# A ConvGLU block on one Trainium2 core: seven column pairs by seven products, and operand halves formed by transfers

## The chip, the cores and the metric

The kernel runs on one core of a Trainium2 chip. Its engines are TensorE (PE, matmuls), VectorE (DVE), ScalarE (ACT), GpSimd (POOL) and SyncE (SP); each runs its own queue of instructions in order, and semaphores order them against each other. Matmul results land in PSUM, everything else in SBUF. Transfers (DMAs) are sent from a queue of SP, POOL or ACT and then run by themselves. The metric is the time of one execution on the device in microseconds (us).

## The reference, cut to what matters

One layer of an encoder block over 512 tokens of width 1024: a combined projection, two attention branches, a gated merge, and a convolutional GLU. The change concerns the last part alone:

```python
def conv_glu(x, w_up, conv_w, conv_b, w_down):        # x: 512 x 1024, normalized
    hid = x @ w_up                                    # 1024 -> 2 * 2816
    hid = causal_depthwise_conv(hid, width=3) + conv_b
    gate, up = hid[..., :2816], hid[..., 2816:]
    return (silu(gate) * up) @ w_down                 # 2816 -> 1024
...
x = x + conv_glu(rms_norm(x, norm2_g), w_ffn_up, ffn_conv_w, ffn_conv_b, w_ffn_down)
```

All of it is in float32, to float32 accuracy. TensorE reads a rounded format (fp32r), so the kernel splits each operand a into a high half hi = round(a) and a low half lo = a − hi, and forms each product as three: hi·hi, hi·lo and lo·hi.

## The kernel before

**Chunks.** The weights come as a list of chunks. `load(i)` sends the transfer of chunk i from SP into a buffer `raw` (two of them); `split_gen(i)` makes `whi` (by ACT's copy) and `wlo` (by DVE's subtraction) of it, sends the load of chunk i + 2 and then yields. `run_chunk` runs the body of one chunk on PE, and at each yield of the body takes one step of the next chunk's split. So PE works on chunk i while ACT and DVE split chunk i + 1 and the load of i + 2 is under way.

**Up projection.** There are 22 column pairs, up0 to up21: 128 gate columns and the 128 up columns that belong to them. An ordinary pair (`up_body`) has 48 matmuls of 128x512. A pair in `SEVEN` (`up_seven`) is computed by Strassen's scheme in Winograd's form: the 1024 x 256 weights and the tokens are cut in two each way, and seven products of blocks take the place of eight, with sums of blocks as operands: 84 matmuls of 128x256. The sums on the token side (`ts`, four tiles, `token_sums`) are made once from a transposed copy that went through DRAM (`htd`); their splits into halves are taken during two ordinary pairs. The sums on the weight side are made for each such pair by DVE: `block_sums` (tile `sx` and one in place in `raw`), and `split_seven` splits them into `wxh` and `wxl`. Partial products are added in `pc`, `hg` and `hu`. Before, `SEVEN` is (5, 8, 11, 14, 17).

**After each pair**, `up_fin` and `gate` apply the convolution (one ACT instruction and two on DVE for each half), silu on ACT into `cg`, and DVE's product into `ub`, which holds four of them.

**Operands of the down projection.** The down projection is computed by seven products as well. For this, each two column pairs 2i and 2i + 1 give an operand pair i (0 to 10): `ax` (the blocks that the first half needs) and `ay` (those of the second). `pair_sums(i)` makes them: four sums of blocks on DVE into `st` (one buffer) and `ub`, then halves: for each part of `ax` and `ay` a cast on ACT into the first half of the tile, and a subtraction on DVE (L909) into the second. The steps of operand pairs 0 to 8 are written right behind `up_fin`. Since SBUF is short, `ay` of pairs 0 to 6 is spilled to DRAM (`ayd`), by a DMA on POOL's queue, and fetched back by `fetch`, also on POOL's queue: five after up18, two inside the down projection.

**Down projection.** The first half, dn0, runs over 11 chunks dn0_0 to dn0_10 of 24 matmuls of 128x512, with `ax`; the second, dn1, over 11 chunks of 18 with `ay`. The weights' own sums are made in `split_down` (in `raw`, kept in t, "t2_..."), first the sums, then the first lo half, the second, and t. A load of dn0_n goes out when chunk n − 2 has let go of its buffer (dn0_2 has one of its own).

**What sets the order.** The code is written for a scheduler that orders each engine's instructions; `behind(a, others)` puts an order between two instructions without a wait, and `chain` does so along a list: in dn0 DVE's and ACT's split work runs along such chains (`late["halves"]`, `late["casts"]`), whose first links (at n = 1) stand behind the last product of up21 (`late["fin"]`) and its last tap. Tiles wait for the last use of the buffer that they take over.

Of the kernel before, what the change touches and what calls it, by code (L numbers as in the profile page):

```python
# [8 lines left out]
F32 = mybir.dt.float32  # L9
# [53 lines left out]
SEVEN = (5, 8, 11, 14, 17)  # L63
# [3 lines left out]
def block_kernel(ctx: ExitStack, tc: tile.TileContext, x, xt, params, g2, rbx, wts, wd0, wd1, out):  # L67
# [45 lines left out]
    def load(i, parts=1):  # L113
# [6 lines left out]
        if i >= FIRST_DN:  # L120
            n = i - FIRST_DN
            if n < NP:
                SP.dma_start(raw, wd0[n])
            else:
                late["load"] = (SP.dma_start(raw[:, 0:1024], wd1[n - NP]),)
            yield
            return

        cuts = [0, *parts, 8] if isinstance(parts, tuple) else [8 * j // parts for j in range(parts + 1)]
        for a, b in zip(cuts, cuts[1:]):  # L130
            sl = slice(256 * a, 256 * b)
            SP.dma_start(raw[:, sl], wts[i, :, sl])
            yield
# [39 lines left out]
    def block_sums(i):  # L173

        b = raws[i].rearrange("p (b c) -> p b c", c=512)
        sx = late["pool"].tile([P, 1536], F32, tag="sx", name=f"sx_{order[i]}")
        late["sx"] = sx
        s1, s2, s4 = (sx[:, 512 * j:512 * (j + 1)] for j in range(3))
        V.tensor_tensor(s1, b[:, 1], b[:, 3], op=ALU.add)
        yield  # L180
        V.tensor_tensor(s2, s1, b[:, 0], op=ALU.subtract)
        yield
        V.tensor_tensor(s4, b[:, 2], s2, op=ALU.subtract)
# [4 lines left out]
    def split_seven(i, raw, hi, lo):  # L188

        key = order[i]  # L190
# [3 lines left out]
        sx = late["sx"]  # L194
        for j, (h, l, src) in enumerate(((hi[:, 0:1024], lo[:, 0:1024], raw[:, 0:1024]),
                                         (wh[:, 0:1024], wl[:, 0:1024], sx[:, 0:1024]),
                                         (hi[:, 1024:2048], lo[:, 1024:2048], raw[:, 1024:2048]),
                                         (wh[:, 1024:1536], wl[:, 1024:1536], sx[:, 1024:1536]))):
            A.copy(h, src)
            V.tensor_tensor(l, src, h.bitcast(F32), op=ALU.subtract)  # L200
            if j < 3:
                yield
# [62 lines left out]
    ayd = dram.tile([7, P, 1536], F32, tag="ayd", name="ayd")  # L265

# [354 lines left out]

    def soft_b(h, t, ps):
# [247 lines left out]
    def pair_sums(i):  # L870
# [5 lines left out]
        if i < 8:  # L876
            ax = fp.tile([P, 2048], F32R, tag="ax", name=f"ax{i}", bufs=8)
            ay = fp.tile([P, 1536], F32R, tag="ay", name=f"ay{i}")
        elif i == 8:

            ax = fp.tile([P, 2048], F32R, tag="ts", name=f"ax{i}", bufs=4)
            ay = fp.tile([P, 1600], F32R, tag="wxh", name=f"ay{i}")[:, 0:1536]
            keep[0] = fp.tile([P, S], F32, tag="hg", name="t2_0")
# [367 lines left out]
```

## Time and profile before

| | |
|---|---|
| median of 3 runs | 726.2 us (725.96 to 726.39) |
| profiled execution | 726.66 us, its span 724.9 us |
| PE / DVE / ACT / POOL busy | 718.6 / 565.4 / 401.5 / 53.6 us |
| up projection, pairs 2 to 21 with the rest of 0 and 1 | 403.0 to 615.8 us |
| down projection, dn0 and dn1 | 615.8 to 675.6 and to 720.8 us |
| transferred | 100.91 MB, 139 GB/s on average |

How to read the rows: a group gives the line of the kernel, the engine, the operation, what it writes and reads with sizes, and how often (x), then busy us in all, mean ns of one, idle time of the engine just before, and what ended that idle time. A row of the chain of waits gives a start in us, a length, and the work. A row of the timeline gives start, length and the work, with idle time ahead of it in brackets; x2 stands for two instructions in one row. A row of transfers gives count, size and the median time from issue to landing. A row of windows gives the busy time of each engine in a stretch, with the granted clock of PE (1.00 is full speed), the busy share of the DMA engines, and GB/s.

### The profile page before, as it was taken

The page shows a single profiled execution, that of the slowest core. Times are in us where ns is not written, and L with a number is a line of the kernel's source. Part 1 is how long each engine was busy: PE and PEld are TensorE (multiplying, and loading weights), DVE is VectorE, ACT ScalarE, POOL GpSimd, SP SyncE. Part 2 cuts the span into 40 slices and gives each one's busy share as a digit, 9 for nine tenths or more (in the row PEclk, how much of TensorE's full clock was granted, in tenths as well). Part 3 has the DMA queues.
Part 4 walks back from the last instruction along what each step waited for, and adds up shares of the span by engine and source line. Part 5 has one row for each costly group of instructions (what it writes and reads, how often), then busy time and mean ns, then how long its engine had stood idle before and what let it go on. Part 6 is the DMA issues. An engine that isn't in the chain of part 4 may idle for free.

```text
span 724.9 us, 10589 instructions
## 1 busy us (share of the span) xinstructions
PE 718.6 (99%) x4019; PEld 627.5 (87%) x4019; DVE 565.4 (78%) x1030; ACT 401.5 (55%) x727; POOL 53.6 (7%) x95
## 2 busy tenths in 40 slices
PE   8999999999999999999999999999999999999997
PEld 8999998888988888888889889889898988888886
DVE  6678867775988888566275799998979985997686
ACT  6675656657767676442254556655545653543541
POOL 2701200000101011000012000000000100000000
PEclk9999999999999999999999999999999999999999
DMA  8632232211313111314536613544335553564563
GB/s 308 250 131 78 83 117 74 74 59 58 118 63 113 59 59 59 136 68 144 195 149 239 203 62 156 186 135 160 118 145 186 181 184 117 173 243 174 177 222 116
DMA packets 24786, 100.91 MB, mean 139 GB/s; under 512 B 2592, under 2 KB 7328, under 8 KB 17184
## 3 DMA queue, kind: packets, MB, share of 16 engines
q1 hardware_dynamic: 21792, 87.00, 33.8%
q0 software_dynamic: 2656, 13.11, 5.0%
q8 instruction: 31, 0.51, 0.3%
q14 instruction: 19, 0.16, 0.1%
q10 hardware_dynamic: 288, 0.14, 0.1%
HBM read 88.44 MB, written 11.80 MB: 138 GB/s over the span
## 4 chain that ended last, share of the span: by engine, by line
PE 98%; DMA 1%; SPq 0%; DVE 0%; ACT 0%; DVEq 0%; issue 0%
PE P L1087 14%; PE p L998 7%; PE pg L254 4%; PE pg L253 4%; PE pg L255 4%; PE pu L254 4%; PE pu L255 4%; PE pu L253 4%; PE qkB L255 2%; PE gB L255 2%; PE qkB L253 2%; PE gA L253 2%; PE gA L254 2%; PE gB L253 2%; PE gA L255 2%; PE qkB L254 2%
## 5 line engine op out<-in xcount | busy, mean ns | idle before, releaser
L253 PE MATMUL pg<-hth,whi_up 128*128 128x512 f32 (+1 forms) x152 | 55.7, 367 | 0.0
L255 PE MATMUL pg<-hth,wlo_up 128*128 128x512 f32 (+1 forms) x152 | 55.7, 366 | 0.0
L254 PE MATMUL pg<-htl,whi_up 128*128 128x512 f32 (+1 forms) x152 | 55.7, 366 | 0.0
L254 PE MATMUL pu<-htl,whi_up 128*128 128x512 f32 (+1 forms) x152 | 55.6, 366 | 0.0
L253 PE MATMUL pu<-hth,whi_up 128*128 128x512 f32 (+1 forms) x152 | 55.6, 366 | 0.0
L255 PE MATMUL pu<-hth,wlo_up 128*128 128x512 f32 (+1 forms) x152 | 55.6, 365 | 0.0
L1087 PE MATMUL P<-whi_dn,ax 128*128 128x512 f32 x176 | 54.4, 389 | 0.0
L149 ACT CAST whi_dn<-raw_dn 128x1024 fp32r<-128x1024 f32 x33 | 34.3, 1051 | 25.5 <-PE P L1087 15.2
L145 DVE TENSOR_TENSOR wlo_dn<-raw_dn,whi_dn 128x1024 fp32r<-128x1024 f32 x33 | 40.0, 1224 | 9.2 <-ACT whi_dn L149 9.1
L228 DVE TENSOR_TENSOR wlo_up<-raw_up,whi_up 128x1024 fp32r<-128x1024 f32 (+1 forms) x40 | 41.2, 1062 | 7.0 <-ACT whi_up L226 7.0
L226 ACT CAST whi_up<-raw_up 128x1024 fp32r<-128x1024 f32 (+1 forms) x40 | 34.5, 917 | 14.7 <-PE pu L254 7.9
L1087 PE MATMUL P<-whi_dn,ay 128*128 128x512 f32 x132 | 40.8, 389 | 0.0
L1087 PEld LDWEIGHTS P<-whi_dn,ax 128*128 128x128 f32 x176 | 33.0, 188 | 6.8
L1087 PE MATMUL P<-wlo_dn,ax 128*128 128x512 f32 x88 | 34.2, 389 | 0.0
L254 PEld LDWEIGHTS pu<-htl,whi_up 128*128 128x128 f32 x152 | 28.6, 188 | 4.7
L253 PEld LDWEIGHTS pu<-hth,whi_up 128*128 128x128 f32 x152 | 28.5, 188 | 4.7
L255 PEld LDWEIGHTS pg<-hth,wlo_up 128*128 128x128 f32 x152 | 28.6, 188 | 4.7
L255 PEld LDWEIGHTS pu<-hth,wlo_up 128*128 128x128 f32 x152 | 28.5, 188 | 4.6
L253 PEld LDWEIGHTS pg<-hth,whi_up 128*128 128x128 f32 x152 | 28.6, 188 | 4.6
L254 PEld LDWEIGHTS pg<-htl,whi_up 128*128 128x128 f32 x152 | 28.6, 188 | 4.5
L633 DVE TENSOR_TENSOR_SCAN aB<-aB,reset 128x127 f32<-128x127 f32 (+3 forms) x32 | 26.0, 817 | 6.7 <-ACT aB L628 6.7
L1087 PEld LDWEIGHTS P<-whi_dn,ay 128*128 128x128 f32 x132 | 24.8, 188 | 5.1
(303 smaller groups left out, 2240.3 us busy)
## 6 DMA issues: line engine op xcount, KB each, us to landing
raw_up<-in_wts SPq DMA_DIRECT2D x22, 1024.0 KB, 4.8
raw_dn<-in_wd SPq DMA_DIRECT2D x11, 1024.0 KB, 4.8
raw_dn<-in_wd SPq DMA_DIRECT2D x11, 512.0 KB, 3.4
ayd<-ay POOLq DMA_DIRECT2D x7, 768.0 KB, 5.2
ay<-ayd POOLq DMA_DIRECT2D x7, 768.0 KB, 6.5
raw_gA<-in_wts SPq DMA_DIRECT2D x4, 1024.0 KB, 4.7
raw_qkB<-in_wts SPq DMA_DIRECT2D x4, 1024.0 KB, 4.8
raw_gB<-in_wts SPq DMA_DIRECT2D x4, 1024.0 KB, 4.7
```

Source lines behind the costliest of these rows:

```text
L145: chain("halves", V.tensor_tensor(o, x, y, op=op))
L149: chain("casts", A.copy(hi[:, sl], src))
L226: A.copy(hi[:, sl], raw[:, sl])
L228: E.tensor_tensor(lo[:, sl], raw[:, sl], hi[:, sl].bitcast(F32), op=ALU.subtract)
L253: PE.matmul(ps, sh, mh, start=first, stop=False)
L254: PE.matmul(ps, sh, ml, start=False, stop=False)
L255: PE.matmul(ps, sl, mh, start=False, stop=last)
L633: V.tensor_tensor_scan(ar, ar, reset[:, S - n:S - 1][:, ::-1], 1.0, op0=ALU.mult, op1=ALU.max)
L998: PE.matmul(ps, st, mv[:, k, :], start=first and k == 0 and n == 0, stop=last and k == 3 and n == 2, skip_group_check=True)
L1087: chain("products", PE.matmul(dst, st, mv, start=first and n == 0, stop=last and n == 2, skip_group_check=True))
```

## The change

It has these parts:

1. `SEVEN` becomes (8, 10, 12, 14, 16, 18, 20), seven pairs; the weights of these are laid out by blocks as the others were.
2. `block_sums` makes one sum in a smaller tile `s1` and one in place in `raw`; the other two are made in place in `raw` inside `split_seven`, between the splits. The splits of the sums are of 512 columns each.
3. `pc` shrinks from three blocks to one; free parts of `hg` and `hu` take the rest.
4. Operand halves of pairs 0 to 8: the low half is no longer a DVE subtraction. ACT copies the source with scale −1 into the place of the low half (rounded as the high half is), and a DMA on POOL's queue adds the source to it (`accum_op=ALU.add`): four more ACT instructions and four DMAs for each operand pair.
5. The steps of `pair_sums`, then six blanks, then the spill of the `ay` of the pair before, go to a list, of which `run_chunk` takes one step at each yield. Spills move from POOL's queue to SP's, ordered behind the last load sent. `ay` has two buffers. `ax` of pair 0 is spilled too (`axd`, 1 MB) and fetched into a `ts` slot after up20; pair 8's operands take ordinary slots.
6. The splits of the token sums move from pairs 2 and 3 to pairs 4 and 5.
7. The fetches of `ay` go out one at a time: after dn0_0 (ay0), dn0_2 (ay1), dn0_3 (ay5), dn0_5 (ay6), dn0_6 (ay2), dn0_8 (ay3) and dn1_0 (ay4), each with a true wait for the landing of the load sent last by then (`after`): dn0_4, 5, 6, 8, 9, dn1_0 and dn1_3.

```diff
-SEVEN = (5, 8, 11, 14, 17)
+SEVEN = (8, 10, 12, 14, 16, 18, 20)
...
     def block_sums(i):
         b = raws[i].rearrange("p (b c) -> p b c", c=512)
-        sx = late["pool"].tile([P, 1536], F32, tag="sx", name=f"sx_{order[i]}")
-        s1, s2, s4 = (sx[:, 512 * j:512 * (j + 1)] for j in range(3))
+        s1 = late["s1"] = late["pool"].tile([P, S], F32, tag="s1", name=f"s1_{order[i]}")
         V.tensor_tensor(s1, b[:, 1], b[:, 3], op=ALU.add)
         yield
-        V.tensor_tensor(s2, s1, b[:, 0], op=ALU.subtract)
-        yield
-        V.tensor_tensor(s4, b[:, 2], s2, op=ALU.subtract)
-        yield
         V.tensor_tensor(b[:, 1], b[:, 0], b[:, 1], op=ALU.subtract)
...
+        part(hi, lo, 0, raw[:, 0:1024])
+        V.tensor_tensor(b[:, 0], s1, b[:, 0], op=ALU.subtract)
+        yield
+        part(wh, wl, 0, s1)
+        part(wh, wl, 512, b[:, 0])
+        yield
+        part(hi, lo, 1024, raw[:, 1024:2048])
+        V.tensor_tensor(b[:, 2], b[:, 2], b[:, 0], op=ALU.subtract)
+        yield
+        part(wh, wl, 1024, b[:, 2])
...
         for _ in body(*splits.pop(key)):
             next(sp, None)
+            if late.get("todo"):
+                late["todo"].pop(0)()
             yield
...
                 A.copy(a[:, sl], src)
-                ins.append(V.tensor_tensor(a[:, n + o:n + sl.stop], src, a[:, sl].bitcast(F32), op=ALU.subtract))
+                if i < 9:
+                    A.activation(lo, src, AF.Copy, scale=-1.0)
+                    G.dma_start(lo, src, accum_op=ALU.add)
+                else:
+                    ins.append(V.tensor_tensor(lo, src, a[:, sl].bitcast(F32), op=ALU.subtract))
...
-            for step in pair_sums(j // 2):
-                step()
-            if j // 2 < 7:
-                G.dma_start(ayd[j // 2], pairs[j // 2][1].bitcast(F32))
+            late["todo"] += [*pair_sums(i), *[lambda: None] * (6 if i else 0)]
+            if 0 < i < 8:
+                late["todo"].append(lambda: behind(SP.dma_start(ayd[i - 1], pairs[i - 1][1].bitcast(F32)), late["ld"]))
+            if i == 6:
+                late["todo"].append(lambda: behind(SP.dma_start(axd, pairs[0][0].bitcast(F32)), late["ld"]))
...
-            if j in (2, 3):
+            if j in (4, 5):
                 next(late["ts"])
...
     def fetch(i):
...
-        G.dma_start(ay, ayd[i])
+        after(G.dma_start(ay, ayd[i]), late["ld"])
...
-        if j == 18:
-            for i in range(5):
-                fetch(i)
+        if j == SEVEN[-1]:
+            keep[0] = fp.tile([P, S], F32, tag="hg", name="t2_0")
+            ax0 = fp.tile([P, 2048], F32R, tag="ts", name="ax0_", bufs=4)
+            G.dma_start(ax0, axd)
+            pairs[0] = (ax0, None)
...
             for _ in run_chunk(f"dn{s}_{i}", down_body(s, i), pieces=2):
                 pass
+            n = ({0: 0, 2: 1, 3: 5, 5: 6, 6: 2, 8: 3}, {0: 4})[s].get(i)
+            if n is not None:
+                fetch(n)
```

What moves in the queues, at three places. First, POOL's queue from the last operand pairs of the up projection on; before, it holds spills into `ayd` and fetches from it:

```order
L933 DMA ayd_108<-ay5_5383 128x1536
L953 DMA ay0_6036<-ayd_108 128x1536
L933 DMA ayd_108<-ay6_5544 128x1536
L953 DMA ay1_6038<-ayd_108 128x1536
L953 DMA ay2_6040<-ayd_108 128x1536
L953 DMA ay3_6042<-ayd_108 128x1536
L953 DMA ay4_6044<-ayd_108 128x1536
L953 DMA ay5_6411<-ayd_108 128x1536
L953 DMA ay6_6494<-ayd_108 128x1536
```

The same stretch of POOL's queue after, from the accumulating transfers of operand pair 8 on (those from `ub` and `st8`):

```order
L918 DMA ay8_6011<-ub_4185 128x256
L918 DMA ax8_6010<-st8_6036 128x256
L918 DMA ax8_6010<-ub_4185 128x768
L918 DMA ay8_6011<-st8_6036 128x512
L1078 DMA ax0__6344<-axd_109 128x2048
L968 DMA ay0_6467<-ayd_108 128x1536
L968 DMA ay1_6550<-ayd_108 128x1536
L968 DMA ay5_6594<-ayd_108 128x1536
L968 DMA ay6_6670<-ayd_108 128x1536
L968 DMA ay2_6708<-ayd_108 128x1536
L968 DMA ay3_6780<-ayd_108 128x1536
L968 DMA ay4_6888<-ayd_108 128x1536
```

The spills have left this queue, four accumulating transfers for each operand pair have come, and the fetch of ax0 stands ahead of all fetches of `ay`. Second, ACT's queue at the end of the up projection, before (pg and pu are the PSUM banks of gate and up columns; L851 is the convolution's tap, L867 silu):

```order
L851 ACTIVATE cg21_6215<-pg21_6180,par_88 128x512
L867 ACTIVATE cg21_6215<-cg21_6215 128x512
L851 ACTIVATE ub_4184<-pu21_6181,par_88 128x512
L149 CAST whi_dn0_1_6266<-raw_dn0_1_6145 128x1024 x2
L908 CAST ay9_6329<-ub_4184 128x256
```

And after, with the same work at L861, L877, L146 and L914:

```order
L861 ACTIVATE cg21_6381<-pg21_6346,par_88 128x512
L861 ACTIVATE ub_4185<-pu21_6347,par_88 128x512
L146 CAST whi_dn0_1_6432<-raw_dn0_1_6265 128x1024 x2
L914 CAST ay9_6497<-ub_4185 128x256
L877 ACTIVATE cg21_6381<-cg21_6381 128x512
```

Silu of cg21 has moved behind the two casts of dn0_1 and the first cast of ay9; on DVE the product that reads it still stands ahead of dn0_1's lo halves. Third, SP's queue from pair 16's load on, before:

```order
L132 DMA raw_up16_5537<-in_wts 128x2048
L132 DMA raw_up17_5598<-in_wts 128x2048
L132 DMA raw_up18_5708<-in_wts 128x2048
L132 DMA raw_up19_5830<-in_wts 128x2048
L132 DMA raw_up20_5875<-in_wts 128x2048
L132 DMA raw_up21_6001<-in_wts 128x2048
```

And after:

```order
L129 DMA raw_up16_5568<-in_wts 128x2048
L945 DMA ayd_108<-ay4_5141 128x1536
L129 DMA raw_up17_5616<-in_wts 128x2048
L129 DMA raw_up18_5785<-in_wts 128x2048
L945 DMA ayd_108<-ay5_5358 128x1536
L948 DMA axd_109<-ax0_4438 128x2048
L129 DMA raw_up19_5834<-in_wts 128x2048
L129 DMA raw_up20_6003<-in_wts 128x2048
L945 DMA ayd_108<-ay6_5575 128x1536
L129 DMA raw_up21_6056<-in_wts 128x2048
```

A spill now stands between loads, behind the load last sent, once for each two loads, and the spill of ax0 with that of ay5.

More of the change, by code (lines that the diff above doesn't have):

```diff
@@ L121, in load @@
             n = i - FIRST_DN
[L122 to L125, printed above, removed]
+            late["ld"] = (SP.dma_start(raw, wd0[n]) if n < NP else SP.dma_start(raw[:, 0:1024], wd1[n - NP]),)
             yield
@@ L131, in load @@
             sl = slice(256 * a, 256 * b)
-            SP.dma_start(raw[:, sl], wts[i, :, sl])
+            late["ld"] = (SP.dma_start(raw[:, sl], wts[i, :, sl]),)
             yield
@@ L620, in behind, with after @@
         return ins
+    def after(ins, others):
+        for o in others:
+            tc.add_manual_dep(ins.ins, o.ins.name, mybir.DependencyInfo(
+                mybir.DependencyClass.Sync, mybir.DependencyReason.DATA), reason="paced")
+        return ins
     def soft_b(h, t, ps):
@@ L1050, in block_kernel @@
     late["ts"] = token_sums()
+    late["todo"] = []
     for j in range(NF):
@@ L1054, in block_kernel @@
             pass
-        if j == 18:
-            for i in range(5):
-                fetch(i)
+        if j == NF - 1:
+            for step in late["todo"]:
+                step()
+            late["todo"] = []
+        if j == SEVEN[-1]:
[3 more added lines that the diff above has]
+            pairs[0] = (ax0, None)
     BLK = {1: 0, 2: 1, 5: 2, 7: 3, 3: 0, 4: 1, 6: 2}
@@ L1179, in steps1 @@
         for t in range(NT):
-            behind(SP.dma_start(tmp["x"][t // 2][:, t % 2, :], x2d[t]), late["load"])
+            behind(SP.dma_start(tmp["x"][t // 2][:, t % 2, :], x2d[t]), late["ld"])
             if t in (1, 2):
```

48 lines of the change are left out of this document (21 added, 27 removed).

## The prediction

> **What bounds the kernel now.** I began with the page's busy times and its chain of waits.
>
> ```profile
> PE 718.6 (99%) x4019; PEld 627.5 (87%) x4019; DVE 565.4 (78%) x1030; ACT 401.5 (55%) x727; POOL 53.6 (7%) x95
> PE 98%; DMA 1%; SPq 0%; DVE 0%; ACT 0%; DVEq 0%; issue 0%
> ```
>
> TensorE (PE) is busy 718.6 of 724.9 us and is 98% of the chain that ended last, so the time is PE's work plus 6.3 us. A change can win only by removing matmul time, and lose only by making PE wait. The chain in order of time prices the two kinds of column pair:
>
> ```profile
> 435.60 9.89 PE p L998 x84
> 467.28 9.89 PE p L998 x84
> ...
> 615.78 104.94 PE P L1087 x462
> ```
>
> A column pair by seven products (L998, 84 matmuls) takes 9.89 us. From 435.60 to 467.28 lie one such and two ordinary ones, so an ordinary one takes (31.68 − 9.89)/2 = 10.89. From 615.78, E below, the down projection runs to the end with no pause. Then I asked how full the other engines are while PE never waits, by two windows (the five periods of 31.68 us from the first seven-product pair, and the first half of the down projection, dn0, 11 chunks):
>
> ```profile
> core 0: us, PE busy (x) PEld busy (x) DVE busy (x) ACT busy (x) POOL busy (x), PEclk, DMA share, GB/s
> 435.60:594.00 158.40, 158.40 (x901) 139.59 (x901) 144.90 (x229) 91.27 (x141) 6.45 (x12) 1.00 0.46 165
> 615.80:675.60 59.80, 59.80 (x265) 49.53 (x265) 52.00 (x67) 29.48 (x36) 1.07 (x2) 1.00 0.55 193
> ```
>
> VectorE (DVE) is busy 28.98 us of each 31.68 (91%), ScalarE (ACT) 18.25 (58%). The granted clock is 1.00 throughout, so matmul times carry over. In dn0 PE takes 59.80/11 = 5.44 us a chunk.
>
> **Two more pairs by seven products.** Five become seven: 2 × (10.89 − 9.89) = −2.0 us of PE. The next pair's first matmul comes some 0.02 us after the last counted, so I take −1.97. The other terms ask whether anything makes PE wait.
>
> **DVE and ACT in the up projection.** The period becomes one ordinary and one seven-product pair: 10.89 + 9.91 = 20.8 us, from pair 8 to 21. These are the rows for it:
>
> ```profile
> L909 DVE TENSOR_TENSOR ax<-ub,ax 128x768 fp32r<-128x768 f32 x9 | 8.6, 955 | 0.0
> L909 DVE TENSOR_TENSOR ay<-st,ay 128x512 fp32r<-128x512 f32 x9 | 6.2, 689 | 0.0
> L909 DVE TENSOR_TENSOR ay<-ub,ay 128x256 fp32r<-128x256 f32 x8 | 3.4, 424 | 0.0
> L909 DVE TENSOR_TENSOR ax<-st,ax 128x256 fp32r<-128x256 f32 x8 | 3.4, 420 | 0.0
> L179 DVE TENSOR_TENSOR sx_up<-raw_up 128x512 f32<-128x512 f32 x4 | 2.8, 688 | 2.9 <-DMA raw_up<-in_wts 2.9
> L200 DVE TENSOR_TENSOR wxl_up<-sx_up,wxh_up 128x1024 fp32r<-128x1024 f32 x4 | 4.9, 1225 | 0.0
> L1010 DVE TENSOR_TENSOR pc<-pc 128x256 f32<-128x256 f32 x5 | 2.1, 423 | 0.0
> ```
>
> ```profile
> L908 ACT CAST ax<-ub 128x768 fp32r<-128x768 f32 x8 | 6.7, 834 | 2.7 <-DVE ub L899 2.7
> L908 ACT CAST ay<-st 128x512 fp32r<-128x512 f32 x9 | 5.6, 620 | 5.7 <-DVE st L901 5.7
> L908 ACT CAST ay<-ub 128x256 fp32r<-128x256 f32 x8 | 3.2, 406 | 6.8 <-DVE ub L928 6.8
> L908 ACT CAST ax<-st 128x256 fp32r<-128x256 f32 x8 | 3.2, 401 | 3.8 <-DVE st L898 3.8
> L199 ACT CAST wxh_up<-sx_up 128x1024 fp32r<-128x1024 f32 x4 | 4.2, 1040 | 1.8 <-DVE sx_up L181 1.8
> ```
>
> A seven-product pair costs DVE over an ordinary one 4 × 0.69 (block sums), 1.23 + 0.69 (splits of the sums) and 5 × 0.42 (adds of products) = 6.8 us. Two thirds of the old period's 28.98 are 19.3; a half instead of a third of the pairs adds a third of 6.8, 2.3; the four L909 subtractions of an operand pair go, −2.5. That is 19.1 of 20.8 us, 92%, as full as before and no fuller. ACT: two thirds of 18.25 are 12.2; a third of the seven's own 3.3 (1.04, 0.62 and four copies of 256 columns at 0.40) adds 1.1; the four negated copies, priced as L908's four casts, add 0.83 + 0.62 + 0.41 + 0.40 = 2.3. Sum 15.6, 75%. Both fit, so no term. The token sums' splits move from pairs 2 and 3 to 4 and 5, ordinary pairs that lose the L909 work: no term. The in-place sums hold a raw buffer until its last split, but I estimate some 19 of 20.8 us for that loop (a load of 4.8, its turn behind the ordinary pair's splits, then sums and splits spread over PE's steps).
>
> **The accumulating transfers.** 36 of them (four a pair, 128 to 384 KB) replace L909; no row shows one. What waits for them is the next sums, which reuse st (one buffer): of the period's 20.8 us some 9 pass from the first sum to the last issue (four sums of 0.42, 4.5 us of casts and negated copies, ACT's other work between), so by estimate the st halves must land within 12 us. The transfers' rows:
>
> ```profile
> raw_up<-in_wts SPq DMA_DIRECT2D x22, 1024.0 KB, 4.8
> ayd<-ay POOLq DMA_DIRECT2D x7, 768.0 KB, 5.2
> ay<-ayd POOLq DMA_DIRECT2D x7, 768.0 KB, 6.5
> ...
> htd<-xf_n POOLq DMA_DIRECT2D x8, 256.0 KB, 3.3
> ...
> raw_up<-in_wts SPq DMA_DIRECT2D x1, 1024.0 KB, 8.8
> ay<-ayd POOLq DMA_DIRECT2D x1, 768.0 KB, 9.0
> ```
>
> Lower end 3.3 us (256 KB from the same queue), upper end 9.0 (three times the bytes beside a load that took 8.8). I take 4 to 6, nearest to 256 KB with an addition; both ends are under 12, so they cost nothing. The spills go to the sync queue (SP): each stands behind a load already sent and reads operands finished a period earlier, so the loads behind it wait for its issue alone. The fetch of ax0 starts within pair 20, some 18 us before dn0 needs it, against 9.0 at the slowest: nothing.
>
> **The start of the down projection.** Here something does move. The gate's last activation (silu of cg21) goes behind the casts of dn0_1 and one of ay9, and DVE's product for pair 21, which waits for it, stands ahead of dn0_1's lo halves:
>
> ```profile
> L867 ACT ACTIVATE cg<-cg 128x512 f32<-128x512 f32 x17 | 10.7, 631 | 13.1 <-DVE cg L854 13.1
> ```
>
> ```profile
> 616.50 1.99 ACT L149 CAST whi_dn<-raw_dn 128x1024 fp32r<-128x1024 f32 x2
> 618.39 0.95 ACT L908 CAST ay<-ub 128x256 fp32r<-128x256 f32 x2
> ```
>
> ```profile
> 618.21 0.69 DVE L928 TENSOR_TENSOR ub<-cg,ub 128x512 f32<-128x512 f32 x1
> 618.82 2.36 DVE L145 TENSOR_TENSOR wlo_dn<-raw_dn,whi_dn 128x1024 fp32r<-128x1024 f32 x2
> ...
> 636.97 0.68 DVE L145 TENSOR_TENSOR t<-raw_dn 128x512 f32<-128x512 f32 x1
> ...
> 642.92 0.68 DVE L145 TENSOR_TENSOR t<-raw_dn 128x512 f32<-128x512 f32 x1
> ...
> 644.73 1.41 DVE L145 TENSOR_TENSOR raw_dn<-raw_dn 128x512 f32<-128x512 f32 x2
> 646.06 2.43 DVE L145 TENSOR_TENSOR wlo_dn<-raw_dn,whi_dn 128x1024 fp32r<-128x1024 f32 x2
> ...
> 649.00 1.41 DVE L145 TENSOR_TENSOR raw_dn<-raw_dn 128x512 f32<-128x512 f32 x2
> 650.33 2.43 DVE L145 TENSOR_TENSOR wlo_dn<-raw_dn,whi_dn 128x1024 fp32r<-128x1024 f32 x2
> ```
>
> The casts end at 618.39, ay9's takes 0.4, silu (L867) 0.6, the product 0.6 (618.21 to 618.82): dn0_1's lo halves start near 620.0 instead of 618.82, and the DVE chain of dn0, busy 52.00 of 59.80 us, runs some 1.2 us later. What PE has in hand: the first lo half of dn0_6 is ready at 646.06 + 1.21 = 647.27, and PE wants it 0.23 into chunk 6, at 615.78 + 6 × 5.44 + 0.23 = 648.65. That lead of 1.4 is about the smallest, and the shift leaves 0.2; dn0_7's, by the row of 650.33, falls from 2.5 to 1.3. The bounds of this term are 0 and, if the shift is half a microsecond larger, 0.3.
>
> **The paced fetches.** Six of seven ay fetches (768 KB) now run in dn0, each sent when a weight load has landed; two did before. The load behind shares the path with them. The two nearest rows (each issue alone in its window):
>
> ```profile
> raw_up<-in_wts SPq DMA_DIRECT2D x1, 1024.0 KB, 7.0
> ...
> raw_dn<-in_wd SPq DMA_DIRECT2D x1, 1024.0 KB, 4.7
> ay<-ayd POOLq DMA_DIRECT2D x1, 768.0 KB, 7.6
> ```
>
> The first, at 557.13, followed a fetch and a spill by 3 us; the second was sent 0.3 us before a fetch, and the fetch alone paid. A load goes out when t of the chunk two earlier is done. Load 7 starts at 642.92 + 0.68 and is used at 649.00, both shifted alike, so it has 5.4 us; load 6, from 636.97 + 0.68 to 644.73, has 7.1; loads 8 to 10, by the rows that follow, about 4.9, under leads of 1.8 and more. Loads of 4.7 cost nothing. Loads of 7.0 make load 7 late by 1.6, against a lead of 1.3: 0.3 us of PE. I take 0.2 for the start and the fetches together, since fetch and load start within half a microsecond, as in the row of 4.7. The Trainium skill, "DMA: Bandwidth & Descriptors", section "Issuing engines are not separate DMA queues", says that transfers started by different engines run on the same 16 DMA engines and interleave. By that rule the load pays as in the row of 7.0, and the sum would end 0.1 us higher; the row of 4.7 doesn't bear it out. The last one (ay4) goes after dn1_3's load, with 5 to 9 us for a transfer of 4.5 to 9.0: nothing, or a few tenths.
>
> **Sum.** 726.66 us for the profiled execution − 1.97 + 0.2 = 724.9; it stands 0.46 above the median of the runs, 726.2, so 724.4 on that basis.
>
> **Rivals.**
> 1. The fetches cost more: loads beside them take 8.8, as the slowest row. Load 6 comes 1.7 late against a lead of 0.2, PE waits 1.5; load 7, 3.4 late against 1.3 + 1.5, adds 0.6. That is 2.1 us and a time of 726.3; at 7.5 it is 0.2 + 0.6 = 0.8 and 725.0. For it: dn0's DMA is at 193 GB/s and gets 3 MB more. Against it: the row of 4.7.
> 2. The other side: accumulating transfers slower than any row. Past 12 us each period loses the excess on DVE, six periods, after some 6 us of PE's lead are used. Slower by over 0.2% needs 3.4 us of waits: 6 × (L − 12) − 6 = 3.4, L = 13.6. At 15 us it is 12 us and 736.2. For it: nothing here shows an addition in a transfer; against it: three times the bytes under full load took 9.0.
> 3. The raw buffers' loop is what runs late. If each load beside a spill takes 7.3 instead of 4.8, the loop is about 21.5 of 20.8 and loses 0.7 in each of six periods, 4 us, under a lead of 6. It reaches PE only if my 19 is short by half a microsecond or more: 6 × 1.2 − 6 = 1.2 us, 725.4, and more with each tenth.
> 4. It saves nothing, as PE was never the bound: excluded, with PE 98% of the chain.
>
> **How the numbers follow.** A measurement of this kernel can tell about 0.2%, 1.45 us: faster is below 724.75, slower above 727.65. The forecast (waits under 0.55 us) gets 0.53; rival 1 0.24, nearly all of it within 0.2%; rival 3 0.11, spread over same and slower; rival 2 0.09; others, as ay4 late or something unseen, 0.03. That makes faster 0.54, same 0.29, slower 0.17. The forecast's own range is 723.9 (no waits, 724.2, less the 0.24 by which the lowest run shown lies under the median) to 724.8. For eight in ten it must take in rival 1 and the near part of rival 3: 723.9 to 727.2.
>
> **What would show it.** Right: 84-matmul rows of 9.89 us seven times, 20.8 us apart; PE busy near 716.6 with no idle between 403 and the end; DVE's subtraction of operand halves for the last two operand pairs alone. Accumulating transfers landing in under 12 us. wlo_dn starting about 4.2 after E instead of 3.04. Wrong: PE idle released by wlo_dn in dn0 with DVE or ACT waiting for raw_dn (rival 1); DVE waiting for a transfer before st (rival 2); whi_up or wlo_up releasing PE with raw_up behind (rival 3). A price I hold firm that could still fail is the rate of matmuls, if it depends on other traffic.

## The result: slower by 1.45%

The changed kernel takes 736.75 us (median of 4 runs, 735.13 to 739.15) against 726.3 (725.96 to 726.94): a ratio of 1.0145, 95% interval 1.0118 to 1.0173. The profiled execution took 739.15 us, its span 737.4, 12.5 above the span before. Busy times and chain of waits of the page after:

```profile
PE 722.1 (98%) x4091; PEld 631.4 (86%) x4091; DVE 560.1 (76%) x1023; ACT 423.6 (57%) x782; POOL 81.6 (11%) x125
PE 61%; DVE 16%; DMA 12%; issue 6%; ACT 2%; SPq 1%; POOL 1%; DVEq 0%; POOLq 0%; ACTq 0%
```

PE alone no longer makes the chain: DVE, transfers and "issue" (waits that the profile explains by nothing) have 34% of it. Where the time went, by the first matmul of each stage in the two traces:

| stretch | before | after | difference |
|---|---|---|---|
| start to first matmul of up2 | 402.77 | 404.94 | +2.2 |
| up2 to up21 | 212.85 | 221.66 | +8.8 |
| dn0 | 59.84 | 61.39 | +1.6 |
| dn1 to the end | 49.48 | 49.45 | 0.0 |

In the second row the saving is inside, so some 11 us are lost there: by the starts of the pairs about 6.8 from up6 to up9, 1.5 in up18, 2.4 in up20 and up21. PE's records have 7.2 us of idle time for it. Another 1.7 goes where PE runs at half its clock for 3.41 us, behind the longest stall (a row of windows; the clock is third from the end):

```profile
474.06:477.47 3.41, 3.37 (x16) 3.37 (x17) 3.41 (x5) 1.37 (x3) 0.88 (x1) 0.50 0.36 55
```

The chain shows what stands behind the later losses (start, length, work):

```profile
562.46 11.49 DMA ay<-st
574.53 4.31 issue
578.86 0.87 POOL ax L918
...
581.87 0.86 POOL ax L918
582.73 4.68 issue
587.42 9.88 DMA ay<-st
```

The two transfers in this piece end a wait of DVE each; between them POOL sends one transfer at a time and stands without a reason that the profile has. The waits of DVE and of ACT show the two places where the up projection stops (total, times, longest):

```profile
DVE st L903 <- DMA ay<-st: 11.6, 4, 6.8
```

```profile
ACT ay L914 <- DMA ayd<-ay: 7.8, 3, 4.6
```

The first is the next operand pair's sum, which takes over st from an accumulating transfer; the second is the cast into an `ay` buffer that waits for a spill. The transfers from 400 us on (count, size, median us to landing). The loads are slower than before (6.4 for 4.8), but the accumulating transfers are by their medians inside the range that the prediction gave them:

```profile
raw_up<-in_wts SPq DMA_DIRECT2D x18, 1024.0 KB, 6.4
...
ayd<-ay SPq DMA_DIRECT2D x7, 768.0 KB, 7.9
...
ax<-ub POOLq DMA_DIRECT2D x9, 384.0 KB, 3.9
ay<-st POOLq DMA_DIRECT2D x9, 256.0 KB, 4.5
```

POOL's timeline tells more. Four sends of operand pairs 0 and 1 (start, length, in brackets the idle time ahead):

```profile
433.36 0.86 POOL L918 DMA_DIRECT2D ax<-ub  x1 [2.17 <-DVE wlo_up L228]
441.82 0.86 POOL L918 DMA_DIRECT2D ay<-st  x1 [7.60 <-issue]
445.40 0.85 POOL L918 DMA_DIRECT2D ay<-ub  x1 [2.72 <-issue]
448.40 0.86 POOL L918 DMA_DIRECT2D ax<-st  x1 [2.15 <-ACT whi_up L226]
```

The first three of these, each alone in a window of the transfers' view (the last number is the time from issue to landing):

```profile
ax<-ub POOLq DMA_DIRECT2D x1, 384.0 KB, 8.2
...
ay<-st POOLq DMA_DIRECT2D x1, 256.0 KB, 3.3
...
ay<-ub POOLq DMA_DIRECT2D x1, 128.0 KB, 2.7
```

433.36 + 8.15 = 441.51, and the next goes out at 441.82; 441.82 + 3.27 = 445.09, next 445.40; 445.40 + 2.69 = 448.09, next 448.40. Each accumulating transfer is sent 0.3 us after the one before it has landed. Its operands don't ask for that: ACT had the source of the second ready at 434.1. Wherever in the trace the next one's operands are ready in time, its send follows that landing by the same 0.3.

### The profile page after: what moved, and what is told of

Read it like the earlier page. It is cut to its first block, busy times and chain, and to the rows that moved or that the text cites. A ratio compares the mean times of both kernels' runs of the same rounds, so it can differ in the third digit from the quotient of the medians.

```text
span 737.4 us, 10930 instructions
## 1 busy us (share of the span) xinstructions
PE 722.1 (98%) x4091; PEld 631.4 (86%) x4091; DVE 560.1 (76%) x1023; ACT 423.6 (57%) x782; POOL 81.6 (11%) x125
## 4 chain that ended last, share of the span: by engine, by line
PE 61%; DVE 16%; DMA 12%; issue 6%; ACT 2%; SPq 1%; POOL 1%; DVEq 0%; POOLq 0%; ACTq 0%
PE P L1109 7%; DMA ay<-st 3%; DMA raw_up<-in_wts 2%; DMA ayd<-ay 2%; DVE wlo_dn L142 2%; PE qkB L257 2%; PE gB L257 2%; PE qkB L255 2%; PE gA L256 2%; PE gA L255 2%; PE gB L255 2%; PE gA L257 2%; PE qkB L256 2%; PE gB L256 2%; DMA raw_dn<-in_wd 2%
## 5 line engine op out<-in xcount | busy, mean ns | idle before, releaser
L255 PE MATMUL pg<-hth,whi_up 128*128 128x512 f32 (+1 forms) x136 | 49.7, 366 | 1.9 <-DVE cg L864 1.9
L146 ACT CAST whi_dn<-raw_dn 128x1024 fp32r<-128x1024 f32 x33 | 34.5, 1051 | 29.1 <-DMA raw_dn<-in_wd 15.5
L257 PE MATMUL pg<-hth,wlo_up 128*128 128x512 f32 (+1 forms) x136 | 49.7, 366 | 0.3 <-DVE wlo_up L228 0.2
L1109 PE MATMUL P<-whi_dn,ax 128*128 128x512 f32 x160 | 49.6, 390 | 0.0
L256 PE MATMUL pg<-htl,whi_up 128*128 128x512 f32 (+1 forms) x136 | 49.5, 364 | 0.0
L256 PE MATMUL pu<-htl,whi_up 128*128 128x512 f32 (+1 forms) x136 | 49.4, 363 | 0.0
L255 PE MATMUL pu<-hth,whi_up 128*128 128x512 f32 (+1 forms) x136 | 49.4, 363 | 0.0
L257 PE MATMUL pu<-hth,wlo_up 128*128 128x512 f32 (+1 forms) x136 | 49.3, 363 | 0.0
L228 DVE TENSOR_TENSOR wlo_up<-raw_up,whi_up 128x1024 fp32r<-128x1024 f32 (+1 forms) x36 | 35.9, 1041 | 4.3 <-ACT whi_up L226 4.3
L226 ACT CAST whi_up<-raw_up 128x1024 fp32r<-128x1024 f32 (+1 forms) x36 | 30.4, 901 | 7.8 <-PE pu L256 4.2
L645 POOL TENSOR_SCALAR_AFFINE_SELECT bB<-bB 128x128 f32<-128x128 f32 x32 | 13.6, 428 | 149.0 <-DVE bB L644 134.3
```

Of the source, the lines that this page charges most:

```text
L146: chain("casts", A.copy(hi[:, sl], src))
L226: A.copy(hi[:, sl], raw[:, sl])
L228: E.tensor_tensor(lo[:, sl], raw[:, sl], hi[:, sl].bitcast(F32), op=ALU.subtract)
L255: PE.matmul(ps, sh, mh, start=first, stop=False)
L256: PE.matmul(ps, sh, ml, start=False, stop=False)
L257: PE.matmul(ps, sl, mh, start=False, stop=last)
```

## The experiments

**The descriptor ring.**

```diff
-    nc = bacc.Bacc(..., dynamic_dma_scratch_size=512)
+    nc = bacc.Bacc(..., dynamic_dma_scratch_size=1024)
```

> The changed kernel with 1024 instead of 512 bytes a partition for the descriptors of POOL's transfers, nothing else. Theory A (the descriptor ring): in the changed kernel each accumulating transfer is sent 0.30 us after the one before it has landed, although no semaphore orders them, because the ring has no room for two of them. Then with twice the room they go out about 1 us apart, three at once, DVE's waits for st (11.6 us in all) fall under 4, the stalls of PE in pairs 18 to 21 (3.9 us) go, and the time is 729 to 733. Rival B (an accumulating transfer waits for the earlier ones by itself, whatever the ring): sends stay behind landings, 736 to 738. Rival C (spills and loads are what is slow, not the sending): sends come closer, but the last st transfer still lands 9 to 11 us after its loads, 734 to 737.

Measured: 727.09 us (725.76 to 731.59, 10 runs), ratio 1.0021 (1.0005 to 1.0036). 9.7 of the 10.5 us lost are back. POOL's timeline in this run, and the two transfers' times:

```profile
443.32 0.84 POOL L918 DMA_DIRECT2D ax<-ub  x1 [3.20 <-ACT ax L917]
444.36 0.85 POOL L918 DMA_DIRECT2D ay<-st  x1 [0.20 <-DVE ub L864]
```

```profile
ax<-ub POOLq DMA_DIRECT2D x1, 384.0 KB, 7.8
...
ay<-st POOLq DMA_DIRECT2D x1, 256.0 KB, 9.3
```

The second is now sent 1.04 us after the first, 6.8 before that lands. The single transfers are as long as before, 9.3 us for one; only the sending changed, so theory A holds, B and C fall, and the gain is more than expected. DVE's waits for st fall from 11.6 to 1.4 us, ACT's for spills from 7.8 to 3.7. In the profiled execution PE has one stall left in the up projection, which costs 1.6 us at up8.

Why two don't fit in 512 bytes can be reckoned from the Trainium skill, as an estimate. "DMA: Bandwidth & Descriptors", sections "Terms" and "The descriptor swizzle", gives 16 bytes for a descriptor and 9 read descriptors for each engine in a transfer to 128 partitions; "Collectives: The Full Stack", section "The bandwidth ceiling: the fold count and why AG ≠ RS ≠ AR", says of the reducing step of a collective that it reads two sources and so takes two read descriptors a chunk. If that holds for an accumulating transfer too, it takes about 17 of the 32 that 512 bytes hold: one accumulating and one plain transfer fit, three plain ones fit, two accumulating ones or four plain ones don't; of 64, three accumulating ones fit and four don't. No trace shows the descriptors, but the sends agree at each point. With 512 bytes the plain fetch of ax0 goes out 0.55 us behind an accumulating transfer in flight, and the kernel before sends three fetches in 1.6 us, while the fourth goes out 0.3 us after the landing of the first at 577.98. With 1024 no trace has more than three accumulating transfers in flight; in the run "Both" below the fourth, its source ready at 485.9, goes out at 486.68, again 0.3 us after a landing.

**The larger ring without the change.** The kernel before with 1024 bytes, as a control.

> The kernel before, with 1024 instead of 512 bytes a partition for the descriptors. A control for the larger ring: its transfers on POOL are plain ones, three of which were sent within 1.6 us already, so nothing changes: 726.0, within 0.5. If the shift of all tiles by 512 bytes or the ring itself changes the pace of PE, it shows here.

Measured: 726.02 us (725.68 to 726.39, 10 runs), ratio 0.9997 (0.9988 to 1.0006), and up2 to up21 takes 212.85 us as before. So the larger ring and the shift of all tiles by 512 bytes don't change PE's pace. They do change the sending of plain transfers, at no gain in time, as PE never waited for them. The fetches of POOL's queue, in the kernel before and in this run:

```profile
572.82 1.61 POOL L953 DMA_DIRECT2D ay<-ayd  x3 [18.37 <-PE p L998]
578.29 0.54 POOL L953 DMA_DIRECT2D ay<-ayd  x1 [3.86 <-PE pg L255]
```

```profile
572.19 2.16 POOL L953 DMA_DIRECT2D ay<-ayd  x4 [20.62 <-PE p L998]
```

**Earlier spills.**

```diff
-            late["todo"] += [*pair_sums(i), *[lambda: None] * (6 if i else 0)]
+            late["todo"] += [*pair_sums(i)]
```

> The changed kernel with no blanks ahead of the spill, so each ay is spilled six steps of PE (about a column pair) earlier. Theory D: the 6.7 us that PE stands in pairs 6 to 9 come from ACT waiting at the cast of ay2 for the spill of ay0, which goes out at 462 and lands at 470; spilled earlier, ACT's waits for ayd (7.8 us) go and the time falls by 3 to 6, 731 to 734. If the serial accumulating transfers alone are the cause (theory A), the waits for ayd go but those for st stay or grow, and the time is 736 to 738.

Measured: 733.51 us (732.54 to 735.48, 4 runs), ratio 1.0105 (1.0086 to 1.0125): 3.2 better than the change, inside what theory D gave. In the changed kernel the spill of ay0 was sent at 462.12, behind a load, and took 7.9 us; ACT's queue and then DVE's stood behind it:

```profile
470.09 0.41 ACT L914 CAST ay<-ub 128x256 fp32r<-128x256 f32 x1 [2.56 <-DMA ayd<-ay]
...
471.76 1.98 ACT L191 CAST whi_up<-raw_up 128x1024 fp32r<-128x1024 f32 x2
```

```profile
472.82 1.23 DVE L192 TENSOR_TENSOR wlo_up<-raw_up,whi_up 128x1024 fp32r<-128x1024 f32 x1 [6.01 <-ACT whi_up L191]
```

up8's weights are cast behind the cast that waits, and PE stands until 472.84. Without the blanks ACT's waits for spills fall from 7.8 to 2.3 us, but the first wait for st, 6.9 us, is still there: there are two causes. They share stalls: alone the ring gives 9.7 us back and the earlier spills 3.2, together 11.0 (next).

**Both.**

> The changed kernel with both: 1024 bytes a partition for the descriptors and no blanks ahead of the spill. With the ring alone one stall of 1.6 us was left in the first seven-product pair (up8), behind ACT's wait for the spill of ay0. Theories A and D together: that stall goes too, PE has no idle time from 403 us to the end, and the time is the forecast of the prediction without its waits: 724.2 (723.8 to 725.2). If other waits take their place (loads of 6.4 us beside the spills): 726 to 728, as with the ring alone.

Measured: 725.74 us (724.92 to 728.14, 11 runs), ratio 0.9996 (0.9987 to 1.0004). From 380 us on PE waits for nothing; the busy times and the last piece of PE's chain are

```profile
PE 717.7 (99%) x4091; PEld 630.4 (87%) x4091; DVE 560.3 (77%) x1023; ACT 423.9 (58%) x782; POOL 81.0 (11%) x125
...
615.56 105.01 PE P L1109 x462
```

up2 to up21 takes 210.63 us, 2.2 less than before: the two pairs save what the sum said. The time is still 1.5 above the 724.2 that the prediction gave for a run without waits, since the start is later, up2 at 404.78 (see below). That cancels the 2.2: no version here is clearly faster than the kernel before. By the ratio to it this one and two that build on it (0.9997 and 0.9999, below) come nearest.

**DVE's subtraction back, in the changed kernel.** No accumulating transfers, ring of 512.

```diff
-                if i < 9:
-                    A.activation(lo, src, AF.Copy, scale=-1.0)
-                    G.dma_start(lo, src, accum_op=ALU.add)
-                else:
-                    ins.append(V.tensor_tensor(lo, src, ...))
+                ins.append(V.tensor_tensor(lo, src, ...))
```

> The changed kernel with the operand halves of all pairs by DVE's subtraction again, so no accumulating transfers and no negated copies; spills, fetches and seven pairs as changed. Theory A (accumulating transfers cost the time, by their serial sending and by what they do to loads): DVE's waits for st vanish, raw_up loads fall from 6.3 to about 5 us; DVE is asked for about 2.5 us more in each 20.8, near its limit, so 724.5 to 730. Rival C (spills on SP and their landing are the cause, through ACT's casts of ay): 733 or more, with ACT waiting for ayd as before.

Measured: 728.2 us (726.83 to 729.01, 10 runs), ratio 1.0025 (1.0016 to 1.0034). Theory A holds in the main: 8.5 us come back without them. One guess in it was wrong: the loads stay at 6.5 us. Either kind of transfer lengthens a load: here one with nothing beside it but a spill sent 0.4 us behind it takes 6.55 us (sent at 454.15), and in the changed kernel one with nothing beside it but an accumulating transfer of 384 KB, sent at almost the same time, takes 6.38 (sent at 433.31). DVE is busy 139.12 us (95%) from up8 on:

```profile
468.25:614.87 146.62, 146.62 (x929) 133.08 (x928) 139.12 (x227) 86.51 (x140) 0.55 (x1) 1.00 0.43 148
```

and PE waits for it only at the end, 1.1 us at the first chunk of dn0 (dn0 takes 61.4 us, against 59.9 with ring and spills mended). So DVE has room in the up projection, where up2 to up21 takes 211.0 us against 210.6, and just too little where dn0 starts. By the medians the transfers, once mended, are 2.5 us better than the subtraction (725.74 to 728.2), but that run has the earlier spills as well; the subtraction with earlier spills was not run.

**Seven pairs alone, and the rest alone.** The kernel before with `SEVEN = (5, 7, 9, 11, 13, 15, 17)`:

> The kernel before with seven pairs by seven products (5, 7, 9, 11, 13, 15, 17) and nothing else of the change: the old sums, DVE's subtractions, POOL's spills and fetches. It asks whether the change's other parts are needed at all. DVE is asked for about 21.6 us in each 20.8: if that is the bound, it loses 0.8 us a period and gains 1.97: 726 to 730 with PE waiting for wlo_up. If DVE's instructions overlap enough, 724.2 to 725. On the start: theory H (a program with seven such pairs starts later, whatever else it has; raw_qA's second part lands after 8 us, and up2 begins up to 2 us later) against chance or the plumbing (lands at 7.1 to 7.5).

Measured: 727.85 us (727.03 to 729.74, 10 runs), ratio 1.0026 (1.0016 to 1.0035). PE stands 1.6 us in the up projection, by its records, and up2 to up21 takes 213.0; the start is late as well, with up2 at 404.81. So the seven pairs alone gain nothing either, and the rest of the change, with ring and spills mended, is worth about 2 us beside them. And the changed kernel with the old five:

> The changed kernel with the old five pairs by seven products (5, 8, 11, 14, 17; token sums split in pairs 2 and 3), ring and spills as changed. If the loss comes from the plumbing (accumulating transfers sent one by one, spills), it stays although nothing is gained: DVE has some 3.7 us less to do in each 31.68, which hides a part, so 728 to 734. If it needs the tighter period of 20.8 us, no loss: 726 to 727.

Measured: 738.51 us (738.3 to 742.43, 4 runs), ratio 1.0184 (1.0159 to 1.0208). All of the loss is there without the tighter period, more than expected: DVE waits 26.9 us for st, and PE 3.0 us at the first chunk of dn0. So the plumbing (accumulating transfers, spills and paced fetches) costs 12 us. That the changed kernel is 1.8 us faster is no clean gain of the two pairs: up2 to up21 takes 221.6 us in this run and 221.7 in that, so in these two traces the added pairs bring as much waiting as they save; this run starts 2.7 us earlier (up2 at 402.25) and loses 1.8 more in dn0.

**The fetches.** In the changed kernel, and with ring and spills mended, the fetches unpaced as before the change, though the five stand after up21 where they stood after up18 (two in dn0, no waits):

> The changed kernel with the fetches of ay as before: five at once after the last column pair, two within dn0, none waiting for a load. Theory E (rival 1 of the prediction, at the end of dn0): PE's 1.5 us in dn0 come from the load sent at 670.48, which takes 9.5 us beside two fetches; those go, but the five fetches fall on the loads of dn0_1 to dn0_3: 735 to 736.5. If the fetches at once delay those loads by more than their lead, 737 to 740.

> As the run with the larger ring and no blanks, and the fetches of ay as before the change (five after the last column pair, two within dn0, none waiting for a load). Theory E': fetches at once fall on the loads of the first dn0 chunks, whose lo halves PE has only 0.2 us in hand for; PE waits 1 to 3 us in dn0, 725.5 to 728. If pacing does nothing, the same time as that run within 0.5 us.

Measured: 738.1 us (735.65 to 739.26, 4 runs), ratio 1.0158 (1.0135 to 1.018); and 725.82 us (725.27 to 727.29, 10 runs), ratio 0.9997 (0.9988 to 1.0006). In the first, dn0 takes 62.4 us against 61.4, so the waits move to earlier chunks rather than go. In the second, dn0 takes 60.4 against 59.9 with paced fetches, PE idle for 0.1 by its records: pacing is worth half a microsecond at most, less than expected. Then ay2 and ay3 after dn0_9 and dn0_10:

```diff
-            n = ({0: 0, 2: 1, 3: 5, 5: 6, 6: 2, 8: 3}, {0: 4})[s].get(i)
+            n = ({0: 0, 2: 1, 3: 5, 5: 6, 9: 2, 10: 3}, {0: 4})[s].get(i)
```

> As the run with the larger ring and no blanks, and the fetches of ay2 and ay3 go out after dn0_9 and dn0_10 in place of dn0_6 and dn0_8. In some executions the load of dn0_10 takes 9.5 us beside the fetches of ay6 and ay2, and PE waits up to 3 us at dn0_10. Theory J: moved to dn1, whose loads are half as large, those two no longer meet the load of dn0_10; dn0 takes 59.9 us in every execution, and the time is 725.2, with the highest run under 727. Rival: the fetches only meet other loads, and the spread stays (725 to 730).

Measured: 726.86 us (725.11 to 728.07, 11 runs), ratio 1.0007 (0.9999 to 1.0016): no better. In the profiled execution, the fastest of the 11, dn0 is clean (59.9) and the load of dn0_10 takes 4.7 us, as theory J said; but ay4 now shares dn1 with them, took 8.5 us, and dn1 is 0.3 us longer. In the run with six pairs at the end of this section, which has the same fetches, PE waits 1.5 us for ay4. The meeting has moved, as the rival said.

**The late start.** What the program does up to 380 us is the same, yet up2 starts 2.2 us later in the changed kernel. After twelve matmuls on the first part of the first weights PE waits for the second part, sent at 2.18 us. Its row among the transfers, with the median to landing as the last number, stands here four times: in the kernel before, in the changed one, and in two kernels below, before with a DRAM buffer added and before with 72 matmuls added:

```profile
raw_qA<-in_wts SPq DMA_DIRECT2D x1, 256.0 KB, 5.0
```

```profile
raw_qA<-in_wts SPq DMA_DIRECT2D x1, 256.0 KB, 6.4
```

```profile
raw_qA<-in_wts SPq DMA_DIRECT2D x1, 256.0 KB, 5.3
```

```profile
raw_qA<-in_wts SPq DMA_DIRECT2D x1, 256.0 KB, 6.1
```

The first suspect was the added DRAM buffer:

```diff
-    axd = dram.tile([P, 2048], F32, tag="axd", name="axd")
+    axd = htd[0:2].rearrange("t b p s -> (t b p s)").rearrange("(p n) -> p n", p=P)
```

> As the run with the larger ring and no blanks, but ax0 is spilled into the first half of htd, which is free by then, in place of a DRAM buffer of its own (axd, 1 MB). In that run PE has no idle time from 403 us on, yet its first ordinary pair starts at 404.8 us against 402.8 before, since the first loads land up to 1.4 us later (raw_qA's second part at 8.4 against 7.1) and PE then runs at a lower clock for a while. Theory F (the place of the inputs in DRAM, moved by the added buffer): the start is as before, and the time 724.0 to 724.5, faster than before by over 0.2%. Rival G (something else of the changed program, such as its size, or chance): 725 to 726 as there.

> The kernel before, with the same DRAM buffer of 1 MB added, and used for one of the seven spills in place of its row of ayd; nothing else. Theory F: its first loads land later and the time is 726.7 to 728, with a wider spread. Rival G: 726.1, spread as before.

Measured: 725.51 us (724.48 to 730.37, 12 runs), ratio 0.9999 (0.9986 to 1.0011), with up2 at 404.73 (its profiled execution is the slowest, 730.37, with 63.3 us in dn0, where the load of dn0_10 takes 9.6 us beside two fetches); and 726.13 us (725.88 to 726.52, 11 runs), ratio 1.0 (0.9992 to 1.0009), with up2 at 402.70. Theory F falls twice. Then the length of PE's program: before with 72 short matmuls behind the last one.

```diff
+    hi, lo = ends[1][1]
+    for _ in range(72):
+        PE.matmul(banks[2][0][:, 0:64], hi[:, 0, 0:128], hi[:, 1, 0:64], start=True, stop=True, ...)
```

> The kernel before with 72 more matmuls of 64 columns behind the last one, as many as two more seven-product pairs add to PE's program; their result is not used. If the length of PE's program is what moves the start, raw_qA's second part lands after 8 us as in all runs with seven such pairs; if not, at 7.1 to 7.5. The end is later by up to 2 us in either case.

Measured: 734.39 us (733.34 to 734.97, 4 runs), ratio 1.0111 (1.0096 to 1.0126). From dn1 on the profiled execution is 5.8 us longer, with those matmuls at its end, where up to 2 were expected; the reading is the start: the load takes 6.1 us and up2 begins at 404.58, though nothing that runs before it was changed. Over all 16 traces: in the four with the program's old length (before, the control with the larger ring, the added buffer, the old `SEVEN`) this load has landed by 7.13 to 7.53 us; in the twelve with 36 to 72 more matmuls at 8.06 to 8.67. The window from 8 to 12 us, first in the kernel before, then in this run (after the length stands PE's busy time with its instructions, the granted clock is third from the end):

```profile
8.00:12.00 4.00, 4.00 (x35) 3.93 (x35) 3.89 (x8) 3.98 (x9) 0.00 (x0) 1.00 1.05 392
```

```profile
8.00:12.00 4.00, 3.25 (x16) 3.26 (x17) 3.01 (x7) 3.71 (x8) 0.00 (x0) 0.62 1.05 396
```

PE does half the matmuls, at a mean clock of 0.62. In the changed kernel's profile this window has 0.73, with ring and spills mended 0.70, in two others 0.60 and 0.63; in these five up2 begins at 404.6 to 404.9. In the seven others with the late load the clock stays at 1.00, and up2 begins at 402.8 to 403.9; in the four with the early load at 402.1 to 402.8. So the start costs about 1 us by the load, and about 1 more where the clock falls.

The fall is one step, 0.50 for 3.41 us, and the length of the wait doesn't tell when it comes: PE stands idle for 1.7 to 2.3 us before the late part in the five, for 1.7 to 2.4 in the seven. What tells is where the wait lies. In the traces' records the granted clock changes only at edges a multiple of 3.41 us apart. In the five PE is busy for less than half of the stretch between two edges in which it waits (0.41 to 0.49 of it), and the clock falls at the end of that stretch; in the eleven others no stretch with a part of the wait has less than 0.50. The run with 72 matmuls, and the one with DVE's subtraction, which just escapes (1.71 busy of 3.41):

```profile
5.57:8.99 3.42, 1.59 (x13) 1.38 (x13) 1.38 (x3) 1.42 (x3) 0.00 (x0) 1.00 0.97 301
8.99:12.40 3.41, 3.41 (x18) 3.41 (x18) 3.15 (x7) 3.41 (x8) 0.00 (x0) 0.50 1.05 390
```

```profile
6.77:10.18 3.41, 1.71 (x14) 1.50 (x13) 1.46 (x4) 1.49 (x4) 0.00 (x0) 1.00 1.04 384
10.18:13.59 3.41, 3.41 (x31) 3.41 (x30) 3.41 (x7) 3.41 (x8) 0.00 (x0) 1.00 1.04 379
```

No run was made to test this reading; later in the traces one stretch of 0.43 (626 us in the run with the old five) had no fall behind it. The Trainium skill, "TensorE: Matmul & The Clock Gate", Part 1, has the clock halved after an idle window of about 3.4 us. The traces agree with the halving and with the 3.41 us, but here PE did not have to be idle for a whole window. Last, six pairs by seven products:

```diff
-SEVEN = (8, 10, 12, 14, 16, 18, 20)
+SEVEN = (10, 12, 14, 16, 18, 20)
```

> As that, with six pairs by seven products (10 to 20). It saves 0.98 us of PE in place of 1.97. If the start is late only beyond some length of PE's program and 36 more matmuls stay under it (raw_qA's second part at 7.1 to 7.5), the time is 724.9 to 725.3; if it goes by degrees or the limit is lower, 725.5 to 726.

Measured: 727.87 us (726.16 to 730.39, 12 runs), ratio 1.0028 (1.0017 to 1.0039), with that load at 6.1 us and up2 at 403.0: 36 more are enough for the late load. The time is above both ranges given; in the profiled execution the wait of 1.5 us for ay4 makes most of that. Why the length of a program, far behind, slows the first loads, no run here shows; that stays open.

## Why the prediction was wrong

The forecast was 724.4 us; the measurement gave 736.75. Term by term:

**Seven-product pairs: right.** 9.89 us each, 20.8 us apart; 2.2 us saved for 1.97 forecast, as the run with ring and spills mended shows.

**DVE and ACT: right.** Neither was the bound. With ring and spills mended DVE is busy 91% of the time from the start of up8 to that of up20, and ACT 71%, for 92% and 75% forecast. With 2.5 us more a period DVE still kept up through the up projection.

**The accumulating transfers: the step that failed.** The sentence "both ends are under 12, so they cost nothing" priced one transfer, from 3.3 to 9.0 us; alone they took 2.7 to 3.9, and at worst 11.5, close to that range. It took for granted that the four of an operand pair run side by side, as the plain fetches of the trace did. They ran one after the other, each send behind the last landing, on a queue where the one that frees st comes last. The nearest rows gave the right time for a transfer and the wrong one for its sending. Rival 2 had the place right (DVE at st, the period's excess) but asked for transfers of 13.6 us; in the event 8.2 us for one in front of another was enough, and 0.09 was too little for it. The 6 us of lead that it allowed PE came from no row.

**The spills: the second step.** The words "so the loads behind it wait for its issue alone" looked at SP's queue. Even there they fall short, since a load with a spill sent behind it took 6.4 to 6.7 us for 4.7 in the run with DVE's subtraction; but with ring and spills mended PE waits for no load in the up projection. The cost was on ACT: the cast into the `ay` buffer waited for the spill's landing, 7.8 us in all, with up8's casts behind it. Earlier spills gave 3.2 us back.

**The start of dn0: right.** wlo_dn of dn0_1 starts 4.3 us after the first matmul of dn0 (626.60); before, it was 3.2 (618.82 after 615.62). The prediction's E is a row of the chain 0.16 later than that matmul, and from there it gave 4.2 for 3.04: the same shift of 1.2 us, within 0.1:

```profile
630.94 1.22 DVE L142 TENSOR_TENSOR wlo_dn<-raw_dn,whi_dn 128x1024 fp32r<-128x1024 f32 x1
```

and PE waited at none of the first chunks; its first wait in dn0 is at 681.7.

**The paced fetches: the size.** 1.5 us for 0.2, in the profiled execution; the same fetches cost nothing in the one with ring and spills mended and 3.4 us in the one with ax0 in `htd`, so the size differs from execution to execution. It was rival 1's mechanism, at another chunk: not loads 6 and 7 but the load of dn0_10, which met two fetches at once:

```profile
raw_dn<-in_wd SPq DMA_DIRECT2D x1, 1024.0 KB, 9.5
ay<-ayd POOLq DMA_DIRECT2D x1, 768.0 KB, 9.3
```

The row of 4.7 on which the term stood was a single fetch sent behind a load; the row of 8.8, with three fetches about, was nearer. The Trainium skill, "DMA: Bandwidth & Descriptors", section "Issuing engines are not separate DMA queues", says that transfers started by different engines run on the same 16 DMA engines and interleave; these two rows, of a load and a fetch that were in flight together, agree.

**The start of the kernel: not in the sum at all.** 2.2 us in the profiled execution, from work that the change doesn't touch.

## What to carry to other kernels

Price a new kind of transfer by its queue, not only by one of its kind: ask how many can be in flight, and look in the trace for sends that follow a landing by a constant time with nothing that the profile can name ("issue"). When a load of work is moved off an engine that had room to spare, its new path must win something else: here DVE kept PE fed through the up projection without it, and lost 1.5 us at the start of dn0. And a gain of 2 us out of 726 can be lost in the start of the program, so compare the stages of two traces one by one before explaining the whole.

## What the hardware showed that was not expected

- With 512 bytes a partition for descriptors one accumulating transfer of 128 rows is in flight at a time, the next sent 0.3 us after its landing, and at most three plain ones; with 1024 up to three accumulating ones, as little as 0.63 us apart, and up to six plain ones. Alone the accumulating ones take 2.7 us for 128 KB, 3.3 for 256 and 3.9 for 384; beside other transfers up to 11.5.
- A load of 1 MB that takes 4.7 us alone takes 6.4 to 6.7 when a spill of 768 KB goes out 0.4 us behind it on the same queue, and 6.4 with an accumulating transfer of 384 KB sent at almost the same time on another. In the kernel before, a plain fetch sent 0.3 us behind a load left the load at 4.7 and took 7.6 itself.
- 72 matmuls added behind the end of the program make the first 256 KB of weights land 1.1 us later (6.1 for 5.0 us).
- A wait of PE of 1.7 to 2.3 us was enough for 3.41 us at half the clock, where less than half of a stretch of 3.41 us was left busy.
